# The low part of split weights: an ACTIVATE and an adding DMA in place of a VectorE subtraction

## The chip, the cores and the metric

The kernel runs on one core of one Trainium2 chip. A core has TensorE (PE, with weight loads listed apart as PEld), VectorE (DVE), ScalarE (ACT), GpSimd (POOL) and SyncE (SP), each with its own queue of instructions in order, and 16 DMA engines that serve the queues of SP, ACT and POOL. The metric is the device time of one execution in microseconds; the profile shows one execution.

## What is computed

One layer of a diffusion block in float32: a modulation, an input projection whose columns go to four mixers (mLSTM, spatial gating, convolution, S5), an output projection with residual and layer norm, and a SwiGLU feed-forward part with a second residual and layer norm. Model width 1024, 1024 latent tokens and 256 context tokens, feed-forward width 2816.

```python
z = h @ w_in_l                                  # h = x * (1 + sc1) + sh1
zc_a = hc @ w_in_l[:, :OFF_B]
zc_d = hc @ w_in_l[:, OFF_D:]
...
y = jnp.concatenate([y_a, y_b, y_c, y_d], axis=-1) @ w_out[l]
x = layer_norm(ALPHA * x + g1 * y, ln1_w[l], ln1_b[l])
x = layer_norm(ALPHA * x + g2 * swiglu(x * (1.0 + sc2) + sh2, w_ffn_in[l], w_ffn_out[l]), ln2_w[l], ln2_b[l])

def swiglu(h, w_in, w_out):
    g, u = jnp.split(h @ w_in, 2, axis=-1)
    return (jax.nn.silu(g) * u) @ w_out
```

## The kernel before

Every large product runs in the float32r format, which holds fewer bits than float32. So weights and activations are each split into a high part (the value cast to float32r) and a low part (the value minus the high part), and each product is three passes: high by high, high weight by low activation, low weight by high activation (`PASSES`). For one block k of the reduction the third matmul is therefore the first that reads the low part of the weights.

**Weights.** `wload` (L843 to L846) loads 512 KB of weights into a buffer called raw; there are two of these. `split2` (L851 to L854) makes the parts: a cast on ScalarE (L853) and a subtraction on VectorE (L854). The parts go to a tile whl, 256 KB for each part; there are four of these slots, and a slot is free again when the last product that reads it has run. In some places the parts go to a page (pg or pg3) and are twice as long, 128 x 1024. `wtile` loads and splits one tile of weights. Where a tile is one of the output weights of the feed-forward part, GpSimd first multiplies raw by the gate g2 in place (L860).

**Projections.** `projT` (L883, L885) gives columns on partitions, and its 128 columns x 8 blocks of k fill two slots; `projK` (L892) gives tokens on partitions, and a pair of its tiles (context keys, context values with gates, latent values with gates, gating) fills all four slots for as long as it runs.

**Output projection.** `out_proj` (L1183) runs for each half of the tokens over two blocks of 512 columns; each block takes four tiles of weights, two in slots and two in pages, through the two raw buffers.

**Feed-forward part.** The first four blocks of 128 columns run as plain projections. After them come nine steps of two blocks each (f = 4, 6, ... 20). In each step `gate_up2` calls `strassen` twice, for the gate weights and for the up weights: seven products of quarters in place of eight, each 12 matmuls, with the seven sums of weights from `a_sums` (L1318 to L1338). `a_sums` works in place in two raw buffers r0 and r1, each of two halves, lo and hi:

```python
yield parts(r0[:, lo])                                    # first product's weights
yield parts(r0[:, hi])                                    # second
v.tensor_tensor(r1[:, lo], r1[:, lo], r1[:, hi], op=ADD)   # L1330
v.tensor_tensor(r0[:, lo], r1[:, lo], r0[:, lo], op=SUB)   # L1331
yield parts(r0[:, lo])                                    # third
v.tensor_tensor(r0[:, hi], r0[:, hi], r0[:, lo], op=SUB)   # L1333
yield parts(r0[:, hi])                                    # fourth
yield parts(r1[:, lo])                                    # fifth
v.tensor_tensor(r1[:, lo], r1[:, hi], r0[:, lo], op=SUB)   # L1336
yield parts(r1[:, lo])                                    # sixth
yield parts(r1[:, hi])                                    # seventh
```

A sum that is written over a half of raw has to come after everything that reads the half as it was. The seven products take turns on three PSUM banks (tag mm) for the gate weights and on the others for the up weights; VectorE adds them up (L1354), the first is copied by ScalarE (L1359), SiLU runs on ScalarE (L1387), and gate times up is formed and split again (L1392 to L1394). Then the second matrix product of the step (L1451) runs with two tiles of output weights, and VectorE adds its results (L1465). After the last two steps one common second product ends the kernel.

**Order of the work.** The program is written as plain code, and a scheduler sets the order within each engine's queue; loads and splits are therefore moved ahead of the products that need them, as far as the buffers allow. `split2` asks for high priority. All loads are issued from SyncE's queue, in order, and a load into raw waits in that queue until raw is free.

Of the kernel before, what the change touches and what calls it, by code (L numbers as in the profile page):

```python
# [27 lines left out]
class Slices:  # L28
    """Small tiles cut from one larger tile."""
# [18 lines left out]
def exp_acc(e, x, shape, cut):  # L48
    """exp(x) to float32 accuracy; returns exp, expm1 of the reduced argument and the power of two."""
# [18 lines left out]
def s5_pre(e, pool, tab):  # L68
    """Everything of the S5 discretization that has one column for each (direction, pair of groups)."""
    nc = e.nc  # L70
    v, a, pe = nc.vector, nc.scalar, nc.tensor
    S = Env()
# [27 lines left out]
    # the phase of one chunk of 8 steps  # L100
# [7 lines left out]
    # powers 0..8 of a_bar: [128, dp, l]  # L108
# [22 lines left out]
    # (a_bar - 1) / lam  # L131
# [18 lines left out]
    # b_bar [128, dp, ri, p] and the same spread block-diagonally over the two groups of a pair  # L150
    S.Bb = pool.tile([128, 2, 2, 8, 16], F32, name="s5Bb")      # d, ri, P, p
# [16 lines left out]
NP = 2      # pairs of groups in a unit  # L168


def s5_unit_tables(e, S, u, tp, wp):
# [3 lines left out]
    # W = a^l b_bar, transposed to [(s p), (gi n)]  # L175
    WT = tp.tile([128, NP, 2, 2, 128], F32, name="s5W", tag="s5W")
    # columns of V, of the Toeplitz matrices and of the result: the steps of a chunk from the last to the first
# [40 lines left out]
    # kernel of the chunk by falling lag, then the Toeplitz matrices through DRAM  # L218
    BD = wp.tile([128, 4, NP, 32], F32, name="s5BD", tag="s5BD")             # (d ri), P, (gi p)
# [24 lines left out]
    for P in range(NP):  # L244
        for gi in range(2):
            # partition (s, p) takes the lags 7 - s and below of row p
            o = gi * 16 * NP * 240 + P * 240
            e.dma(M[:, P, gi, :], bass.AP(tensor=dr.tensor, offset=dr.offset + o, ap=[[16, 8], [NP * 240, 16], [1, 128]]))
    # rotation table
    Ec, Es = (tp.tile([128, 2, NP, 160], F32, name=f"s5E{x}") for x in "cs")  # L250
    for d in range(2):
# [9 lines left out]
        # cos = 1 - 2 sin(pi f)^2, sin = 2 sin(pi f) (1 - 2 sin(pi f / 2)^2)  # L261
# [66 lines left out]
def s5_out(e, Yg, y0, yT, gw, gb, wp):  # L328
    """Yg [c, 7 - t, (g q)] -> y0 (two halves), yT [128 ch, 2, 1024] with the gated linear unit"""
# [20 lines left out]
HO = (0, 2, 1, 3)       # heads as the partitions of a pair lie: (half, pair)  # L350


def mlstm_consts():
    """[104, ...] tables that depend on shapes alone: rows (head, chunk in scan order), 0..39 and 64..103"""
# [19 lines left out]
def mlstm_gates(e, Gk, page, kp):  # L374
    """Gk [128 tok, 10, 16]: gate inputs with their bias, chunks of context then latents"""
# [56 lines left out]
    G.dec = kp.tile([128, 2, 2, 10], F32, name="mdec")       # (half k), pair, direction, step  # L432
# [36 lines left out]
    G.TW = kp.tile([128, 3, 2, 40], F32, name="mTW")         # exp of: e, inter weight, -m  # L469
# [5 lines left out]
def mlstm_states(e, G, kxc, vxc, kT, vx, C, wp):  # L475
    """states before each latent chunk; context in token layout [128, 2, 256], [128, 2, 4, 65]; latents kT, vx"""
# [45 lines left out]
def mlstm_chunk(e, G, c, qT, kT, vx, hb, wp):  # L522
    """latent chunk c of both directions -> hb [128, 4, 64]"""
# [57 lines left out]
def mlstm_norm(e, hb, sq, c0, nw, sig, yT, wp, NC=4):  # L581
    """hb [128, NC, 4, 64] of chunks c0.. -> yT[:, :, tokens] = norm * weight * sigmoid(o)"""
# [23 lines left out]
def sgu_consts(e, lnb, bsb, wsT, B):  # L606
    """the bias image [(2 groups) 64 c, 2, t] from the transposed spatial weights [s, g, t]"""
# [9 lines left out]
def ln_stats(e, srcs, wp, tag, n):  # L617
    """mean and 1/std of each source row ([128, n] each) -> [128, len, 2]"""
# [12 lines left out]
def sgu_norm(e, gv, c0, wp):  # L631
    """gv [128 tok, 8, 256], chunks c0 to c0 + 3, in place"""
    mv = ln_stats(e, [gv[:, c0 + i] for i in range(4)], wp, "g", 256)
    for i in range(4):
        g = gv[:, c0 + i]
        e.nc.vector.tensor_scalar(g, g, mv[:, i, 0:1], mv[:, i, 1:2], op0=SUB, op1=MUL)


def sgu_mix(e, vn, h, wsT, B, lnw, yT, wp):
    """yT [128, 2, 1024], which holds gelu(u), times (w_s vn * ln_w + B), chunks 4 h to 4 h + 3"""  # L640
# [15 lines left out]
def conv_sums(e, wc, ws):  # L656
    """per channel: weights of the even taps plus those of the odd taps, [128, 2, 16]"""
# [5 lines left out]
def conv_taps(e, ap, j, wc, ws, bcol, p0, p1):  # L663
    """ap [128 ch, 16 rows, 96] (already twice the gated input) -> its first 64 columns, in place.

    Even and odd steps apart, with w0 the even and w1 the odd taps, and x+ one step on:
    y even = w0 * x even + w1 * x odd, y odd = (w0 + w1) * (x odd + x even+) - w0 * x even+ - w1 * x odd."""
# [16 lines left out]
def conv_norm(e, x, y, q, lnw, lnb, wp):  # L684
    """x [128 ch, 2, 16, 96], y [128 ch, 2, 1024] over it, tokens of quarter q -> silu(layer norm over the 256 channels)"""
# [24 lines left out]
PASSES = ((0, 0), (0, 1), (1, 0))       # (part of the weight, part of the activation): hi hi, hi lo, lo hi  # L710
# [10 lines left out]
def layout(x):  # L721
    """The inputs as the kernel reads them: transposed, cut into tiles, repeated; no arithmetic."""
# [5 lines left out]
    # S5: partitions (group in its pair, state)  # L728
# [11 lines left out]
    tile_ = lambda w: w.reshape(-1, 128, w.shape[1]).transpose(1, 0, 2)             # [128, k, columns]  # L740
# [21 lines left out]
def body(tc, A, out):  # L762
# [5 lines left out]
    with st:  # L768
# [18 lines left out]
        # ---- constants and small parameters  # L787
# [13 lines left out]
        # ---- modulation: the columns of sh1, sc1 for both streams  # L801
        ccol = cp.tile([128, 16], F32, name="ccol")
        a.activation(ccol, cols[:, 0:16], AF.Silu)          # (stream, k)
# [38 lines left out]
        # ---- weights: loaded, then split into two parts that float32r carries exactly  # L842
# [8 lines left out]
        def split2(hi, lo, r):  # L851
            with tc.high_priority():
                a.copy(hi, r)  # L853
                v.tensor_tensor(lo, r, hi.bitcast(F32), op=SUB)  # L854
# [670 lines left out]
```

## Time and profile before

| What | Value |
|---|---|
| median of 3 runs | 1218.36 us (1217.72 to 1219.31) |
| span of the profiled execution | 1216.7 us |
| granted TensorE clock, mean | 0.987 |
| L853, cast to the high part, 128 x 512 | 228 times, 621 ns, 140.3 us |
| L854, subtraction, pages of 128 x 1024 | 13 times, 1383 ns, 17.9 us |
| DMA queue of GpSimd | 272 packets, 0.70 MB |
| DMA queue of SyncE | 34722 packets, 100.95 MB |

The profile takes one execution apart. The span reaches from the first to the last instruction; the median is of runs without that profile. Busy time is the union of an engine's instructions. A row of a group gives the line, the engine, the operation, output and inputs with their shapes, a count after x, then busy us and mean ns, then the idle time just before the group's instructions and what ended it. A row of the timeline gives start and length in us. Matmuls are pipelined, so that one is listed as longer than the distance to the next.

### The profile page before, as it was taken

To read this page: it belongs to the slowest core of one execution; us is meant where nothing else is said; L and a number is where in the kernel's file an instruction comes from. 1 tells how busy PE (TensorE), PEld (TensorE's weight loads), DVE (VectorE), ACT (ScalarE), POOL (GpSimd) and SP (SyncE) were. 2 spreads that over 40 slices of the span, in tenths; PEclk is the share of its full clock that TensorE was granted. 3 is DMA by queue.
4 is the path that set the end of the run, shared out by engine and by line. 5 is a ranking of instruction groups with operands and counts; after the bars stand their busy time and mean duration, and the time that the engine had idled before them with its cause. 6 is when DMAs were issued, how large, how long until landed. Compare 5 with 4: busy or idle time off the path is not lost.

```text
span 1216.7 us, 15421 instructions
## 1 busy us (share of the span) xinstructions
PE 1170.0 (96%) x5803; PEld 922.9 (76%) x5803; DVE 968.2 (80%) x1902; ACT 419.5 (34%) x688; POOL 71.3 (6%) x52
## 2 busy tenths in 40 slices
PE   6999999999999999999999999999999999999987
PEld 1487788668897778678888787878787878788875
DVE  6588999988998899886866858586867676768786
ACT  1554444422336343752213132322222222323332
POOL 0010000000000000000300101010101010100110
PEclk9999999999999999999999999999999999999989
DMA  9442101121323464620111111121212121211222
GB/s 361 190 141 93 33 34 54 44 83 38 117 71 122 141 206 156 239 73 18 52 35 52 53 43 61 35 69 35 70 36 69 35 70 35 69 35 35 86 88 105
DMA packets 35213, 102.92 MB, mean 85 GB/s; under 512 B 3841, under 2 KB 8097, under 8 KB 34754
## 3 DMA queue, kind: packets, MB, share of 16 engines
q1 hardware_dynamic: 34722, 100.95, 25.2%
q8 instruction: 46, 0.75, 0.3%
q0 software_dynamic: 272, 0.70, 0.2%
q10 hardware_dynamic: 144, 0.29, 0.1%
q14 instruction: 29, 0.24, 0.1%
HBM read 96.17 MB, written 5.75 MB: 84 GB/s over the span
## 4 chain that ended last, share of the span: by engine, by line
PE 74%; DVE 17%; DMA 4%; ACT 2%; issue 2%; POOL 0%; DVEq 0%; SPq 0%; ACTq 0%; POOLq 0%
PE mm L1349 14%; PE mm L883 12%; PE mm L1451 8%; PE a L1451 6%; PE mm L1183 5%; PE b L1349 4%; PE b L1451 4%; PE b L883 4%; PE mm L892 3%; DVE whl L854 2%; PE c L1349 2%; DVE pg L1394 2%; PE c L1451 2%; DVE hs L1354 2%; DVE pg L1392 2%
## 5 line engine op out<-in xcount | busy, mean ns | idle before, releaser
L853 ACT CAST whl<-raw 128x512 fp32r<-128x512 f32 (+1 forms) x236 | 145.5, 622 | 380.6 <-PE mm L1451 153.2
L854 DVE TENSOR_TENSOR whl<-raw,whl 128x512 fp32r<-128x512 f32 (+1 forms) x236 | 165.4, 706 | 109.0 <-ACT whl L853 107.9
L883 PE MATMUL mm<-pg,whl 128*128 128x512 f32 x816 | 216.4, 404 | 0.7 <-ACT pg L1206 0.3
L883 PEld LDWEIGHTS mm<-pg,whl 128*128 128x128 f32 x816 | 146.5, 188 | 37.7 <-issue 6.1
L1349 PE MATMUL mm<-pg,whl 128*128 128x512 f32 x756 | 172.8, 389 | 0.0
L1349 PEld LDWEIGHTS mm<-pg,whl 128*128 128x128 f32 x756 | 141.9, 188 | 29.4
L1349 PE MATMUL b<-pg,whl 128*128 128x512 f32 x504 | 118.1, 389 | 0.0
L860 POOL TENSOR_TENSOR raw<-raw,g 128x1024 f32<-128x1024 f32 x22 | 61.7, 2805 | 852.4 <-DMA raw<-in_w_dram 737.0
L1349 PEld LDWEIGHTS b<-pg,whl 128*128 128x128 f32 x504 | 94.6, 188 | 19.6
L1451 PE MATMUL mm<-whl,pg 128*128 128x512 f32 x372 | 101.0, 400 | 0.0
L1451 PEld LDWEIGHTS mm<-whl,pg 128*128 128x128 f32 x372 | 72.3, 194 | 15.5
L1451 PE MATMUL a<-whl,pg 128*128 128x512 f32 x216 | 59.0, 404 | 12.8 <-DVE pg L1394 9.4
L892 PE MATMUL mm<-whl,pg 128*128 128x256 f32 (+1 forms) x448 | 63.1, 288 | 0.0
L1354 DVE TENSOR_TENSOR pg<-pg,mm 128x512 f32<-128x512 f32 x72 | 47.7, 683 | 19.0 <-PE mm L1349 18.6
L1451 PEld LDWEIGHTS a<-whl,pg 128*128 128x128 f32 x216 | 41.0, 192 | 26.1 <-DVE pg L1394 11.6
L1349 PE MATMUL c<-pg,whl 128*128 128x512 f32 x252 | 60.5, 389 | 0.0
L892 PEld LDWEIGHTS mm<-whl,pg 128*128 128x128 f32 x448 | 58.1, 190 | 1.5 <-issue 1.1
L1451 PE MATMUL b<-whl,pg 128*128 128x512 f32 x216 | 54.8, 389 | 0.0
L1349 PEld LDWEIGHTS c<-pg,whl 128*128 128x128 f32 x252 | 47.3, 188 | 9.8
L1183 PE MATMUL mm<-whl,pg 128*128 128x512 f32 x192 | 50.2, 398 | 0.3 <-DVE pg L1171 0.3
L1183 PE MATMUL mm<-pg 128*128 128x512 f32 x192 | 49.6, 401 | 0.1
L1451 PEld LDWEIGHTS b<-whl,pg 128*128 128x128 f32 x216 | 40.6, 188 | 8.4
(452 smaller groups left out, 1789.1 us busy)
## 6 DMA issues: line engine op xcount, KB each, us to landing
raw<-in_w_dram SPq DMA_DIRECT2D x66, 512.0 KB
pg<-in_wm_dram SPq DMA_DIRECT2D x16, 512.0 KB
raw<-in_wo_dram SPq DMA_DIRECT2D x16, 512.0 KB
raw<-in_wt_dram SPq DMA_DIRECT2D x14, 512.0 KB
mw<-in_w_mod_dram SPq DMA_DIRECT2D x24, 256.0 KB
vx<-in_w_mod_dram SPq DMA_DIRECT2D x24, 256.0 KB
pg<-in_x_dram SPq DMA_DIRECT2D x4, 1024.0 KB
pg<-in_w_mod_dram SPq DMA_DIRECT2D x8, 512.0 KB
```

Of the source, the lines that this page charges most:

```text
L853: a.copy(hi, r)
L854: v.tensor_tensor(lo, r, hi.bitcast(F32), op=SUB)
L860: gp.tensor_tensor(raw, raw, scale, op=MUL)
L883: pe.matmul(ps[h], lhsT=W(wi, k), rhs=rhs(hi, h, k), **f)
L892: pe.matmul(ps, lhsT=lhs(hi, k), rhs=Ws[k // 4](wi, k % 4), start=(k == 0 and n == 0), stop=(k == 7 and n == 2))
L1183: pe.matmul(ps, lhsT=Yr(hi, half, k)[:, t * 128:(t + 1) * 128], rhs=Ws[k // 2](wi, k % 2), start=(i + n == 0), stop=(i == 7 and n == 2))
L1349: pe.matmul(ps, lhsT=W[:, wi, k, :], rhs=B[b][hi][:, k], start=(k + n == 0), stop=(k == 3 and n == 2))
L1354: v.tensor_tensor(o, x, ps, op=ADD)
L1392: v.tensor_tensor(s_, c, s_, op=MUL)
L1394: v.tensor_tensor(lo(i, h), s_, hi(i, h).bitcast(F32), op=SUB)
L1451: pe.matmul(ps, lhsT=G[i][hi][:, t * 128:(t + 1) * 128], rhs=W[i // 2](wi, i % 2), start=(i + m == 0), stop=(i == n - 1 and m == 2))
```

## The change

In `split2` the subtraction on VectorE is replaced by two steps. ScalarE writes the negative of the high part into the low part's place, and a DMA issued from GpSimd's queue adds the raw weights to it (`accum_op=ADD`: the destination is read, added to and written back). This holds for all 249 splits of weights: 236 into slots and 13 into pages. The split of the activations is as before.

```diff
         def split2(hi, lo, r):
+
             with tc.high_priority():
                 a.copy(hi, r)
-                v.tensor_tensor(lo, r, hi.bitcast(F32), op=SUB)
+                a.activation(lo, hi.bitcast(F32), AF.Copy, scale=-1.0)
+                gp.dma_start(lo, r, accum_op=ADD)
```

Nothing else in the code differs but comments. Behind this place the changed kernel's lines have numbers that are higher by 2: its cast is L854, the negative L855, the DMA L856, and L1336 becomes L1338. The scheduler orders the queues anew. Three places of the same steady step (one of the later ones) show what stands where; rows give line, operation, output and inputs, and in brackets whose signals the instruction waits for (DMASW is a DMA from GpSimd's queue, DMAHW one from SyncE's).

ScalarE, from the copy of the first gate product to the first SiLU, before (the three casts are those of the fifth, sixth and seventh weight sum):

```order
L1359 COPY pg_8331<-mm_8361 128x512 [waits PE_49,Activation_49]
L853 CAST whl_8351<-raw_8334 128x512 [waits DMAHW0_49,Activation_49]
L853 CAST whl_8355<-raw_8334 128x512 [waits DVE_49,PE_49,Activation_49]
L853 CAST whl_8358<-raw_8334 128x512 [waits PE_49,Activation_49]
L1387 ACTIVATE pg_8331<-pg_8331 128x512 [waits DVE_49]
```

The same place in the changed kernel:

```order
L1361 COPY pg_8529<-mm_8566 128x512 [waits PE_49]
L854 CAST whl_8553<-raw_8532 128x512 [waits DMAHW0_49,DMASW3_49]
L855 ACTIVATE whl_8553<-whl_8553 128x512 [waits Activation_49]
L854 CAST whl_8558<-raw_8532 128x512 [waits DMASW4_49,DVE_49,PE_49]
L854 CAST whl_8562<-raw_8532 128x512 [waits DMASW5_49,PE_49]
L855 ACTIVATE whl_8558<-whl_8558 128x512 [waits Activation_49]
L855 ACTIVATE whl_8562<-whl_8562 128x512 [waits Activation_49]
L1389 ACTIVATE pg_8529<-pg_8529 128x512 [waits DVE_49]
```

Each split has two instructions on ScalarE now, and the negative of the sixth sum stands behind the cast of the seventh.

VectorE, around the sixth sum of the gate weights, before:

```order
L854 TENSOR_TENSOR whl_8348<-raw_8332,whl_8348 128x512 [waits Activation_49]
L854 TENSOR_TENSOR whl_8351<-raw_8334,whl_8351 128x512 [waits PE_49,Activation_49]
L1336 TENSOR_TENSOR raw_8334<-raw_8334,raw_8332 128x512 [waits DVE_49]
L854 TENSOR_TENSOR whl_8355<-raw_8334,whl_8355 128x512 [waits Activation_49]
L1354 TENSOR_TENSOR pg_8331<-pg_8331,mm_8388 128x512 [waits PE_49]
L854 TENSOR_TENSOR whl_8358<-raw_8334,whl_8358 128x512 [waits Activation_49]
```

The same place in the changed kernel:

```order
L1467 TENSOR_TENSOR pg_4105<-pg_4105,mm_8498 128x512 [waits PE_49]
L1338 TENSOR_TENSOR raw_8532<-raw_8532,raw_8530 128x512 [waits DMASW7_49,Activation_49]
L1356 TENSOR_TENSOR pg_8529<-pg_8529,mm_8593 128x512 [waits PE_49]
L1356 TENSOR_TENSOR pg_8529<-pg_8529,mm_8580 128x512 [waits DVE_49]
L1356 TENSOR_TENSOR pg_8529<-pg_8529,mm_8609 128x512 [waits PE_49]
```

The subtractions are gone from the queue, and the sixth sum, which waited for VectorE's own work, waits for the DMA of the fifth.

TensorE, the start of the sixth gate product, before:

```order
L1349 MATMUL mm_8434<-pg3_5229,whl_8355 128x512 [waits DVE_49,Activation_49]
L1349 MATMUL mm_8434<-pg3_5230,whl_8355 128x512
L1349 MATMUL mm_8434<-pg3_5229,whl_8355 128x512 x2
L1349 MATMUL mm_8434<-pg3_5230,whl_8355 128x512
L1349 MATMUL mm_8434<-pg3_5229,whl_8355 128x512 x2
```

The same place in the changed kernel:

```order
L1351 MATMUL mm_8639<-pg3_5303,whl_8558 128x512 [waits DVE_49,Activation_49]
L1351 MATMUL mm_8639<-pg3_5304,whl_8558 128x512
L1351 MATMUL mm_8639<-pg3_5303,whl_8558 128x512 [waits DMASW0_49]
L1351 MATMUL mm_8639<-pg3_5303,whl_8558 128x512
L1351 MATMUL mm_8639<-pg3_5304,whl_8558 128x512
```

The third matmul, the first that reads the low part, now has a wait of its own, on the DMA. On GpSimd's queue the DMAs of a step's splits stand in the order of the sums, with the two multiplications by g2 (L862) between the last of one step and the first of the next, each ahead of its own tile's DMAs. On SyncE's queue a load into raw now also waits for the DMAs that read the buffer before.

## The prediction

> **What bounds the kernel now.** I read the page's table of engines first, then the chain that ended last, then busy time by stretch. Of the engine rows the reader needs name, busy time and share.
>
> ```profile
> span 1216.7 us, 15421 instructions
> PE 1170.0 (96%) x5803; PEld 922.9 (76%) x5803; DVE 968.2 (80%) x1902; ACT 419.5 (34%) x688; POOL 71.3 (6%) x52
> PE 74%; DVE 17%; DMA 4%; ACT 2%; issue 2%; POOL 0%; DVEq 0%; SPq 0%; ACTq 0%; POOLq 0%
> 30.00:515.00 485.00, 475.26 (x2837) 367.02 (x2836) 429.63 (x1073) 213.73 (x355) 7.77 (x21) 0.99 0.33 109
> 515.00:1145.00 630.00, 616.27 (x2680) 503.83 (x2679) 461.88 (x626) 182.21 (x294) 51.18 (x18) 0.99 0.16 50
> ```
>
> In the last two rows the first pair of numbers is the stretch and its length, then busy time of PE, PEld, DVE, ACT and POOL, the granted clock, the DMA share and GB/s. TensorE is the bound: it idles 485.00 - 475.26 = 9.7 us in the mixers and projections and 630.00 - 616.27 = 13.7 us in the feed-forward part. VectorE carries 17% of the chain but is rarely what TensorE waits for. So unloading VectorE can win back part of these 23 us and no more, while a weight part that comes late is paid in full. The profiled execution is 1216.7 us of span; the median shown, 1218.36, lies 1.7 us above it, and I add every difference to the median.
>
> **What is exchanged.** Groups by shape, with mean ns after the busy time, then issues from GpSimd's queue (last number: us from issue to landing) and one such issue on POOL.
>
> ```profile
> L854 DVE TENSOR_TENSOR whl<-raw,whl 128x512 fp32r<-128x512 f32 x228 | 159.6, 706 | 108.7 <-ACT whl L853 107.6
> L853 ACT CAST pg<-raw 128x1024 fp32r<-128x1024 f32 x13 | 13.6, 1050 | 21.3 <-POOL raw L860 8.9 <-DMA raw<-in_wo_dram 7.4 <-PE a L531 4.3
> L1387 ACT ACTIVATE pg<-pg 128x512 f32<-128x512 f32 x36 | 22.8, 633 | 33.6 <-DVE pg L1354 33.1
> s5gw<-in_s_glu_w_dram POOLq DMA_DIRECT2D x1, 256.0 KB, 3.3
> gw<-in_sgu_wt_dram POOLq DMA_DIRECT2D x1, 256.0 KB, 4.5
> gbs<-in_sgu_bb_dram POOLq DMA_DIRECT2D x1, 128.0 KB, 2.7
> wc<-in_conv_t_dram POOLq DMA_DIRECT2D x1, 31.0 KB, 7.1
> 225.13 0.58 POOL L1126 DMA_DIRECT2D gw<-in_sgu_wt_dram  x1
> ```
>
> VectorE loses 228 subtractions of 0.706 us, 160 us with the few of other shapes beside. ScalarE gains as many passes of about 0.63 us (the row of an ACTIVATE on the same shape), some 145 us; at 419.5 us busy it has room. POOL gains 249 issues of about 0.58 us, 144 us. None of these sums is a term: what counts is how late the low part is ready. Before, it was the cast and the subtraction, 1.3 us. Now it is the cast, the pass, and L, the time from the issue of the adding DMA to its landing. No row shows a DMA that adds. The nearest is gw: 256 KB, 128 rows of 2 KB, same queue, 4.5 us. The other 256 KB row says 3.3; the opening's crowded queues gave 7.1 for 31 KB. An addition also reads its destination, which speaks for the upper side. I take **L = 4.5**, and keep 3.3 to 6.5.
>
> **The feed-forward blocks.** One product-of-quarters in the steady state, in order of time (start, length, engine, line):
>
> ```profile
> 891.53 19.20 PE L1349 MATMUL mm<-pg,whl 128*128 128x512 f32 x84
> 894.99 0.62 ACT L853 CAST whl<-raw 128x512 fp32r<-128x512 f32 x1
> 896.38 0.69 DVE L1336 TENSOR_TENSOR raw<-raw 128x512 f32<-128x512 f32 x1
> 897.22 0.62 ACT L853 CAST whl<-raw 128x512 fp32r<-128x512 f32 x1 [1.60 <-PE mm L1349]
> 899.95 0.62 ACT L853 CAST whl<-raw 128x512 fp32r<-128x512 f32 x1 [2.11 <-PE mm L1349]
> 900.61 0.69 DVE L854 TENSOR_TENSOR whl<-raw,whl 128x512 fp32r<-128x512 f32 x1
> 904.79 0.69 DVE L1330 TENSOR_TENSOR raw<-raw 128x512 f32<-128x512 f32 x1 [0.79 <-DMA raw<-in_w_dram]
> 910.58 2.88 PE L1349 MATMUL b<-pg,whl 128*128 128x512 f32 x12
> 915.36 0.69 DVE L1336 TENSOR_TENSOR raw<-raw 128x512 f32<-128x512 f32 x1
> 919.80 2.79 POOL L860 TENSOR_TENSOR raw<-raw,g 128x1024 f32<-128x1024 f32 x1 [55.43 <-DMA raw<-in_w_dram]
> ```
>
> 84 matmuls take 910.58 - 891.53 = 19.05 us, 0.227 each. The cast at 894.99 is that of the fifth of seven weight sums. The sixth sum (L1336) is written over the fifth's raw half, so in the changed kernel VectorE may start it only when the fifth's DMA has landed; the DVE rows of the order show that wait. Then follow, on ScalarE as its order has them, the cast of the sixth, of the seventh, and the negative of the sixth. In numbers: 894.99 + 0.62 + 0.63 = 896.24; + L; + 0.69 + 0.62 + 0.62 + 0.63 = 898.80 + L; the sixth's DMA lands at 898.80 + 2L. The sixth product's third matmul, the first to read the low part, is due after 62 matmuls, at 905.59. Late by 2L - 6.8: 2.2 us at 4.5, nothing below 3.4.
>
> The seventh's DMA lands at 899.43 + 2L and frees the second raw buffer. Its reload took 904.79 - 901.30 = 3.49 us. Two sums (1.38), cast and pass (1.25) and L again: 905.55 + 3L, for a matmul due at 910.58 + 26 x 0.227 = 916.48. That is 3L - 10.9 = 2.6, so 0.4 more. The second half of the pair (the up weights) repeats the first path, 2.2 less that 0.4. A pair costs 2(2L - 6.8) = 4.4 us, and there are nine: **+40** (0 at 3.3, 112 at 6.5). VectorE's additions that free PSUM banks stand behind the waiting sum; at 4.5 the fifth product would get its bank some 0.4 us late, inside the same stall. The scaled tile of the output weights that follows is hidden: its reload starts with the second half's sixth sum, 3.46 + 1.25 + L + 0.69 after 910.58; reload 3.75 (916.05 to 919.80), scaling 2.79, cast and pass 1.25, L: 13.2 + 2L = 22.2, when the products of that half, delayed, end at 19.05 + 2.2 and a wait of 1.35 (below) stands between. On POOL the scaling waits behind the DMA issues, 0.58 each, and they behind it, in the same cover.
>
> A stall can also cost clock. The same wait before the second matrix product is followed by two different clocks (seventh number from the end of a row's busy times: 0.72 and 1.00):
>
> ```profile
> 806.00:812.00 6.00, 5.95 (x19) 4.77 (x20) 3.86 (x7) 1.24 (x2) 0.00 (x0) 0.72 0.30 90
> 869.00:875.00 6.00, 5.13 (x23) 4.25 (x24) 5.45 (x10) 1.25 (x3) 0.00 (x0) 1.00 0.37 126
> 932.11 1.69 PE L1451 MATMUL a<-whl,pg 128*128 128x512 f32 x5 [1.35 <-DVE pg L1394]
> ```
>
> 6 x 0.28 = 1.7 us where it happens. Eighteen stalls, half of them: **+15** (0 to 31). The last row is also the gain: VectorE ends this 1.35 us wait in each of nine blocks, with subtractions of 0.69 us standing in its queue just ahead. One taken out each time: **-6**; all of it and the mixers' idle 9.7 would be -22.
>
> **Output projection.** A column block takes four slots and two pages through two raw buffers.
>
> ```profile
> 443.33 2.67 ACT L853 CAST whl<-raw 128x512 fp32r<-128x512 f32 x4 [8.13 <-issue]
> 445.40 1.69 SPq L845 DMA_DIRECT2D raw<-in_wo_dram  x2
> 450.26 1.05 ACT L853 CAST pg<-raw 128x1024 fp32r<-128x1024 f32 x1
> 453.97 2.35 DVE L854 TENSOR_TENSOR pg<-raw,pg 128x1024 fp32r<-128x1024 f32 x2
> 349.14 15.34 PE mm L892 x127
> ```
>
> The first page's low part was ready at 455.2 (453.97 and half of 2.35). Now: 443.33, ScalarE's four or six passes until the first buffer's last negative (2.5 to 3.8, say 3.1), L, reload 450.26 - 445.40 = 4.86, cast and pass 2.1, L: 453.4 + 2L, late by 2L - 1.8 = 7.2. TensorE reaches these pages about then, and SyncE's next loads queue behind the waiting reload. Three such block changes: **+22** (14 to 34). Context and token projections hold all four slots to their end; the last row gives 0.121 us per matmul, 24 of them 2.9 us. The first slot is free after 0.7, then 1.25 + L, against 2.9 + 0.9 where the next projection's low part is first read: L - 1.85 = 2.7, four times (context keys, context values, latent values, gating), **+11** (6 to 19). Elsewhere the 10.9 us (48 x 0.227) that a projection works on two slots cover it.
>
> **The last block.** Four scaled weight tiles pass two raw buffers and a scaling on POOL:
>
> ```profile
> 1141.98 0.62 ACT L853 CAST whl<-raw 128x512 fp32r<-128x512 f32 x1
> 1143.36 0.69 DVE L1336 TENSOR_TENSOR raw<-raw 128x512 f32<-128x512 f32 x1
> 1148.03 2.57 POOL L860 TENSOR_TENSOR raw<-raw,g 128x1024 f32<-128x1024 f32 x1 [95.36 <-DMA raw<-in_w_dram]
> 1151.71 1.23 DVE L854 TENSOR_TENSOR pg<-raw,pg 128x1024 fp32r<-128x1024 f32 x1 [0.56 <-ACT pg L853]
> 1156.71 2.39 POOL L860 TENSOR_TENSOR raw<-raw,g 128x1024 f32<-128x1024 f32 x1 [1.52 <-DMA raw<-in_w_dram]
> 1163.17 2.08 PE L1451 MATMUL mm<-pg,pg 128*128 128x512 f32 x4 [2.20 <-DVE pg L854]
> ```
>
> TensorE waits here already. New: 1141.98 + 1.25 + L + 0.69; + 3.98 (1144.05 to 1148.03); + 2.57 + 2.1 + L; + 3.77 (1152.94 to 1156.71); + 2.39 + 2.1 + L = 1160.8 + 3L against 1163.17: 11.2, less 2.2 counted above, **+9** (8 to 11).
>
> Sum: 40 + 15 - 6 + 22 + 11 + 9 = +91; 1218.4 + 91 = **1309 us**.
>
> **Rivals.** (a) Faster. If L is below 3.4 the nine pairs cost nothing, no stall lowers the clock, and the waits on VectorE of 1.35 us go: 9 x 1.35 = 12, and with half the mixers' idle 17; if the handovers too are covered by other products, 1201 us. For it: gbs landed in 2.7, s5gw in 3.3, and the source now lies on the chip. Against it: gw's 4.5 and the doubled reading. The Trainium skill (DMA: Bandwidth & Descriptors, Anatomy of one DMA) gives this path about 2.0 us plus bytes over 436 GB/s, an estimate of 2.6 us for 256 KB, and so this rival; the trace's 3.3 and 4.5 disagree. Chance 0.08. (b) Hidden anyway: L near 3.3, where the stalls left (14 + 6 + 8) are met by gains of up to 22: about 1219 to 1224. Chance 0.06. (c) Worse than the forecast: the additions share the DMA engines with the 512 KB reloads that they themselves release, L goes past 6.5, and the terms give 112 + 31 + 34 + 19 + 11 = 207 or more: above 1425. For it: 7.1 us under load; against: a DMA share of only 0.16 in the feed-forward part. Chance 0.12. (d) The work does not leave VectorE in effect: its queue stands still at the four sums of each half, waiting for DMAs. That is inside the forecast, and would show as wait, not as busy time.
>
> **How the numbers follow.** Forecast 0.74. Low end: 1212, below case (b) and into (a); high end: 1425, L = 6.5 with every stall. Left out: most of (a) and (c), under 0.2. A difference of 0.2%, 2.4 us, is about what a measurement here can tell. Faster 0.08, same 0.04, slower 0.88.
>
> **What would show it.** DVE busy down by about 180 us, ACT up by about 150. Adding DMAs landing in 4 to 5 us. TensorE waiting on DMA at the sixth product of each half, 2 us, and on page tiles in the output projection, 7 us. Wrong if TensorE's idle stays below 60 us, if adding DMAs land under 3.4 us, or if the stalls lie in the third or fourth product instead.

## The result, and the profile after

The changed kernel takes 1312.49 us (median of 4 runs, 1311.84 to 1315.33) against 1218.04 us for the kernel before in the same series (4 runs, 1214.99 to 1219.31): a ratio of 1.0778, 95% interval 1.0757 to 1.08. The forecast was 1309.

First the page after: the engines, GpSimd's DMA queue, and two groups that carry the change (columns as before).

```profile
span 1310.9 us, 16179 instructions
...
PE 1197.3 (91%) x5803; PEld 929.2 (71%) x5803; DVE 777.5 (59%) x1653; ACT 559.6 (43%) x937; POOL 278.2 (21%) x301
...
q0 software_dynamic: 36128, 69.52, 31.0%
...
L856 POOL DMA_DIRECT2D whl<-raw x236 | 203.4, 918 | 863.9 <-ACT whl L855 451.8
...
L1338 DVE TENSOR_TENSOR raw<-raw 128x512 f32<-128x512 f32 x18 | 12.5, 693 | 118.1 <-DMA whl<-raw 118.1
```

The work moved as it should: VectorE lost 191 us, ScalarE gained 140, GpSimd 207. But VectorE now stands 118 us at the sixth sum. TensorE's idle time, span less busy, grew from 1216.7 - 1170.0 = 46.7 to 1310.9 - 1197.3 = 113.6 us; the other 27 us of the 94 are busy time of the same 5803 matmuls. The clock explains some 13 of these (mean granted clock 0.987 before and 0.978 after: 1310.9 x 0.022 - 1216.7 x 0.013). The rest goes with the number of stops, as worked out further below: the last matmul ahead of a wait is listed as longer than one within a row.

Where do they lie? The next view is busy time by stretch, cut at the same places of the program (the counts in brackets differ by up to 15 matmuls, since the order does): up to the output projection; the output projection; the first blocks of the feed-forward part; seven Strassen steps; the last two steps with the end. Before:

```profile
0.00:370.10 370.10, 354.37 (x2102) 259.47 (x2103) 320.63 (x893) 144.33 (x260) 9.60 (x30) 0.99 0.31 106
370.10:495.30 125.20, 122.41 (x685) 98.57 (x684) 111.93 (x266) 57.12 (x78) 0.00 (x0) 0.99 0.45 148
495.30:641.00 145.70, 142.60 (x644) 114.39 (x643) 113.81 (x117) 56.07 (x79) 14.33 (x4) 1.00 0.26 85
641.00:1081.50 440.50, 427.73 (x1850) 349.86 (x1849) 320.07 (x464) 117.90 (x196) 36.85 (x14) 0.99 0.17 51
1081.50:1216.70 135.20, 122.92 (x529) 100.58 (x527) 101.81 (x168) 44.08 (x75) 10.53 (x4) 0.96 0.23 78
```

After:

```profile
0.00:390.90 390.90, 358.65 (x2117) 263.64 (x2118) 293.59 (x847) 169.06 (x308) 51.35 (x78) 0.98 0.48 130
390.90:534.90 144.00, 129.46 (x676) 101.49 (x675) 92.71 (x235) 70.45 (x100) 19.24 (x23) 0.95 0.71 188
534.90:686.60 151.70, 144.54 (x637) 115.44 (x636) 94.31 (x97) 70.59 (x103) 29.08 (x26) 0.98 0.50 127
686.60:1156.10 469.50, 436.39 (x1850) 347.45 (x1850) 221.51 (x340) 188.69 (x324) 143.00 (x141) 0.99 0.56 118
1156.10:1310.90 154.80, 128.22 (x529) 101.19 (x527) 75.41 (x137) 60.81 (x105) 35.48 (x34) 0.95 0.53 126
```

The stretches grow by 20.8, 18.8, 6.0, 29.0 and 19.6 us, 94.2 in all. In each, idle time is the length less the first busy number: in the seven steps 440.50 - 427.73 = 12.8 before and 469.50 - 436.39 = 33.1 after.

Now one half of a steady step in the timeline after, in order of time. The product at 1021.87 starts the gate weights' seven, the cast at 1025.27 is the fifth sum's.

```profile
1021.87 14.21 PE L1351 MATMUL mm<-pg,whl 128*128 128x512 f32 x62
...
1025.27 0.62 ACT L854 CAST whl<-raw 128x512 fp32r<-128x512 f32 x1
1025.92 0.63 ACT L855 ACTIVATE whl<-whl 128x512 fp32r<-128x512 f32 x1
...
1026.85 0.85 POOL L856 DMA_DIRECT2D whl<-raw  x1 [2.35 <-ACT whl L855]
...
1030.24 0.69 DVE L1338 TENSOR_TENSOR raw<-raw 128x512 f32<-128x512 f32 x1 [7.49 <-DMA whl<-raw]
...
1032.98 1.74 POOL L856 DMA_DIRECT2D whl<-raw  x2 [5.28 <-PE mm L1351]
...
1036.04 0.86 POOL L856 DMA_DIRECT2D whl<-raw  x1 [1.32 <-ACT whl L855]
...
1036.30 5.29 PE L1351 MATMUL mm<-pg,whl 128*128 128x512 f32 x22 [0.22 <-DMA whl<-raw]
...
1037.24 0.86 POOL L856 DMA_DIRECT2D whl<-raw  x1 [0.34 <-ACT whl L855]
...
1043.32 0.69 DVE L1332 TENSOR_TENSOR raw<-raw 128x512 f32<-128x512 f32 x1 [3.13 <-DMA raw<-in_w_dram]
...
1049.79 0.50 PE L1351 MATMUL b<-pg,whl 128*128 128x512 f32 x1 [2.31 <-DMA whl<-raw]
```

In the view by tile, the two reloads of raw in these 29 us (duration of the issue, then first and last start):

```profile
L845 SPq DMA_DIRECT2D raw<-in_w_dram x2: 328/328/328, 1031.0 to 1038.0; - x2
```

This is the chain that the prediction described. The fifth's negative ends at 1026.55, its DMA is issued by 1027.70, and the sixth sum can start at 1030.24: L = 3.7 us, issue included. The sixth's and seventh's DMAs follow (1032.98), and after 62 matmuls the sixth product waits a mere 0.22 us. But the seventh's DMA also frees the second raw buffer. Its reload is issued at 1038.0 and is there at 1043.3, 5.3 us where 3.49 were planned: the additions for the first two sums of the next half, issued at 1036.04 and 1037.24, move on the same DMA engines, whose busy share is 0.86 in this stretch (last number but one):

```profile
1036.00:1043.30 7.30, 7.08 (x32) 5.80 (x32) 2.24 (x4) 2.19 (x4) 1.71 (x2) 1.00 0.86 178
```

This holds for all seven steps: the reload with two additions issued just ahead of it takes 4.1 to 6.4 us, the other half's reload, with none ahead of it, 3.5 to 3.8. So the third sum comes late, and the third product of the up weights waits 2.31 us.

### The profile page after: what moved, and what is told of

Read it like the earlier page. It is cut to its first block, busy times and chain, and to the rows that moved or that the text cites. A ratio compares the mean times of both kernels' runs of the same rounds, so it can differ in the third digit from the quotient of the medians.

```text
span 1310.9 us, 16179 instructions
## 1 busy us (share of the span) xinstructions
PE 1197.3 (91%) x5803; PEld 929.2 (71%) x5803; DVE 777.5 (59%) x1653; ACT 559.6 (43%) x937; POOL 278.2 (21%) x301
## 3 DMA queue, kind: packets, MB, share of 16 engines
q0 software_dynamic: 36128, 69.52, 31.0%
q1 hardware_dynamic: 34722, 100.95, 22.8%
## 5 line engine op out<-in xcount | busy, mean ns | idle before, releaser
L856 POOL DMA_DIRECT2D whl<-raw x236 | 203.4, 918 | 863.9 <-ACT whl L855 451.8
L854 ACT CAST whl<-raw 128x512 fp32r<-128x512 f32 (+1 forms) x236 | 142.8, 619 | 423.5 <-PE mm L1453 110.4
L885 PE MATMUL mm<-pg,whl 128*128 128x512 f32 x816 | 217.8, 406 | 5.9 <-DVE pg L1210 4.0
L1351 PE MATMUL mm<-pg,whl 128*128 128x512 f32 x756 | 176.3, 391 | 9.1 <-DMA whl<-raw 7.7
L855 ACT ACTIVATE whl<-whl 128x512 fp32r<-128x512 f32 (+1 forms) x236 | 145.1, 629 | 4.5
L1351 PE MATMUL b<-pg,whl 128*128 128x512 f32 x504 | 125.6, 401 | 16.9 <-DMA whl<-raw 16.2
L1338 DVE TENSOR_TENSOR raw<-raw 128x512 f32<-128x512 f32 x18 | 12.5, 693 | 118.1 <-DMA whl<-raw 118.1
L1351 PE MATMUL c<-pg,whl 128*128 128x512 f32 x252 | 64.7, 405 | 9.3 <-DMA whl<-raw 8.8
L894 PE MATMUL mm<-whl,pg 128*128 128x256 f32 (+1 forms) x448 | 66.1, 294 | 6.3 <-DMA whl<-raw 6.3
L862 POOL TENSOR_TENSOR raw<-raw,g 128x1024 f32<-128x1024 f32 x22 | 55.6, 2528 | 16.7 <-DMA raw<-in_w_dram 15.3
```

What stands on the lines that cost most here:

```text
L855: a.activation(lo, hi.bitcast(F32), AF.Copy, scale=-1.0)
L856: gp.dma_start(lo, r, accum_op=ADD)
L862: gp.tensor_tensor(raw, raw, scale, op=MUL)
L885: pe.matmul(ps[h], lhsT=W(wi, k), rhs=rhs(hi, h, k), **f)
L894: pe.matmul(ps, lhsT=lhs(hi, k), rhs=Ws[k // 4](wi, k % 4), start=(k == 0 and n == 0), stop=(k == 7 and n == 2))
L1351: pe.matmul(ps, lhsT=W[:, wi, k, :], rhs=B[b][hi][:, k], start=(k + n == 0), stop=(k == 3 and n == 2))
```

## The experiments

Each ran in a series beside the kernel before; differences are between medians of one series, and ratios have their 95% interval. "Steps" are the seven Strassen steps, 440.5 us before and 469.5 after, as cut above; each such length is from one profiled execution.

**Which splits cost.** The adding DMA for the Strassen sums alone, and for the other tiles alone; elsewhere VectorE subtracts as before. The new argument says whether a split takes the negative and the DMA; the diff is that of the first run, and the second has the two values exchanged.

```diff
-                split2(x[:, 0], x[:, 1], r)
+                split2(x[:, 0], x[:, 1], r, True)
-                split2(hl[:, 0], hl[:, 1], raw[:, k:k + n])
+                split2(hl[:, 0], hl[:, 1], raw[:, k:k + n], False)
```

> The negative and the adding DMA only for the sums of weights in the Strassen steps (126 of the 249 splits); all other tiles are split by VectorE as before. Theory: the nine steps' own stalls stay and nothing else. In the changed kernel's trace the program's landmarks move by 29.0 us over the first seven steps and by 15.5 over the last two, so 1218 + 44 = about 1262, at least 1250. Rival (contention: additions of all kinds slow each other and the reloads): half of the additions cost clearly less than this, below 1245, and the two halves of the change together come to far less than its whole.

> The opposite: the negative and the adding DMA for all tiles of weights (projections, output projection, scaled output weights), VectorE's subtraction for the Strassen sums. Theory: opening and mixers 20 us, output projection 20, first blocks of the feed-forward part 6, last block 4, by the shifts of the landmarks in the changed kernel, so about 1268; the steps of the feed-forward part keep their old length of 62.9 us. Rival (the scaled tiles of output weights are not hidden in a step, but carry the steps' loss): steps of 65 us or more and 1280 or more.

The sums alone took 1280.98 us against 1220.58, ratio 1.0496 (1.0472 to 1.052), +60.4; the tiles alone 1259.11, ratio 1.0316 (1.0284 to 1.0348), +38.5. Together 98.9, close to the whole's 94.5: the two add up, with no large cost that needs both. But each missed its number: 60 us where 44 were forecast, and 38 where 50 were. The steps say why, with the sums alone:

```profile
645.40:1125.20 479.80, 437.36 (x1850) 348.68 (x1849) 243.62 (x367) 172.43 (x296) 119.46 (x113) 0.99 0.46 100
```

and with the tiles alone:

```profile
690.60:1121.40 430.80, 423.17 (x1850) 347.50 (x1849) 304.70 (x436) 134.91 (x224) 58.52 (x42) 1.00 0.27 69
```

The sums lengthen the steps by 39 us, and the tiles, which in a step are the scaled output weights, shorten them by 10. In the whole change 29 is what is left. A gain was hidden in it.

**The gain by itself.** The adding DMA only for the 28 splits of scaled output weights of the first seven steps; and the same 28 on GpSimd with no DMA.

```diff
-            return wtile(A["w2"][c, :, f0:f0 + 2], 2, 512, scale=bc(g2[:, None, cs_], [128, 2, 512]), pool_tag=tag)
+            return wtile(A["w2"][c, :, f0:f0 + 2], 2, 512, scale=bc(g2[:, None, cs_], [128, 2, 512]), pool_tag=tag, other=4 <= f0 < NFF - 4)
```

> VectorE subtracts everywhere but in the 28 splits of scaled output weights of the first seven Strassen steps, where the negative and the adding DMA stay. The run with all tiles by DMA had steps of 57 to 62 us, 11 us shorter in all than before, and lost its 50 us ahead of the steps. Theory (these tiles are covered in a step, and VectorE's shorter queue ahead of the second product is worth 1.6 us a step): 1219 - 11 = about 1208, at least faster than before by 4 us. Rival (the shorter steps there came from a cooler clock after slower mixers, or from the order of the last blocks): 1215 to 1225.

> GpSimd subtracts for the 28 splits of scaled output weights of the first seven Strassen steps, VectorE does all others; no DMA adds anything. Theory (in these steps it counts only that VectorE's queue is shorter, how the low part is made does not): as the run that gave these 28 splits to the adding DMA, 1206 us within 3. Rival (GpSimd's 1.5 us beside VectorE's work slow VectorE, as its subtraction of the sums may have): 1211 or more.

1206.16 us against 1220.75, ratio 0.989 (0.9869 to 0.991); and 1207.5 against 1220.36, ratio 0.989 (0.9873 to 0.9906). **Both are faster than both kernels**, by 1.1%. How the low part is made there makes no difference; that four subtractions a step are gone from VectorE's queue does. The steps of the first run:

```profile
643.80:1069.70 425.90, 421.38 (x1849) 346.25 (x1848) 303.16 (x436) 134.59 (x224) 59.67 (x42) 1.00 0.27 70
```

and in its timeline the wait ahead of one second matrix product, 1.35 us before:

```profile
865.03 1.43 PE L1456 MATMUL a<-whl,pg 128*128 128x512 f32 x5 [0.56 <-DVE pg L1399]
```

14.6 us shorter than before: 8.3 of idle time and 6.3 of busy time. Of the latter 5.1 are clock: before, it drops three times in the steps behind that wait, at 1.7 us each, and here not once.

**The chain in the sums.** One run takes the fifth's DMA out of the sixth sum's way; the other leaves the DMA to the first four sums and gives the three at the chain's head back to VectorE (all tiles too). Their edits, one after the other:

```diff
-            v.tensor_tensor(r1[:, lo], r1[:, hi], r0[:, lo], op=SUB)
-            yield parts(r1[:, lo])
+            v.tensor_tensor(r0[:, lo], r1[:, hi], r0[:, lo], op=SUB)
+            yield parts(r0[:, lo])
...
-            yield parts(r0[:, hi])
-            yield parts(r1[:, lo])
+            yield parts(r0[:, hi], True)
+            yield parts(r1[:, lo], False)
```

> The whole change, but the sixth sum is written over r0's lower half (the third sum, long read) in place of r1's. So it waits no longer for the fifth's DMA, and r1, whose last reader is the seventh, comes free some 4 us earlier; r0 comes free later instead. Theory (the steps lose by the chain fifth DMA, sixth sum, sixth DMA, seventh DMA, reload of r1): the two stalls of a step that lie on it, at the sixth product and at the third of the second half, go, and with them most of the 43 us that the sums cost: 1312 down to 1270 to 1285, steps of 62 to 63.5 us in place of 67.1. Rival (every adding DMA is late for its own product or slows the reloads, whatever it is chained to): 1300 or more.

> The negative and the adding DMA only for the first four of the seven weight sums of each product (72 of the 249 splits); VectorE subtracts the other three and all tiles. Theory (a chain of three landings, fifth, sixth or seventh, and the third sum of the next half, crosses from one half into the next; no single one is late): r1 comes free as early as before, and the third sum's low part, one landing later than before, is still 5 us ahead of its matmul: 1213 to 1226, where all seven cost 60 us. Rival (each addition is late for its own product, or slows the reloads): four sevenths of 60, 1245 or more.

The first run took 1308.37 us, ratio 1.072 (1.0696 to 1.0744): by its own number the theory had failed. TensorE's waits in the steps (us, times, longest) in the changed kernel:

```profile
PE b L1351 <- DMA whl<-raw: 9.1, 7, 2.3
PE c L1351 <- DMA whl<-raw: 8.8, 4, 3.3
PE mm L1351 <- DMA whl<-raw: 4.9, 7, 1.5
```

and in this run:

```profile
PE a L1453 <- DMA whl<-raw: 11.1, 7, 1.6
PE a L1453 <- ACT pg L1395: 9.9, 7, 2.0
PE b L1351 <- DMA whl<-raw: 3.5, 5, 0.9
```

The waits inside the products did go, from 22.8 us to about 5, but the second matrix product now waits for its scaled tile and for ScalarE: r0 comes free later, and what is loaded into it is late instead. In all, idle time in the steps fell only from 33.1 to 28.3 us, and the clock took that back: its drops cost 13.6 us in place of 5.1 (1.7 each, as shown further below; mean granted clock 0.97, third number from the end, in place of 0.99).

```profile
693.00:1163.10 470.10, 441.77 (x1850) 353.68 (x1850) 243.18 (x340) 192.62 (x324) 143.46 (x141) 0.97 0.56 118
```

The waiting was for the most part shifted, not saved. The second run answers the question: 1219.95 against 1218.65 us, ratio 1.0006 (0.9987 to 1.0025), with 72 adding DMAs in place of the 126 that cost 60 us alone; the idle time in its steps is 12.8 us, as before. Four sevenths of the additions cost nothing; the loss needs the last three sums and the landing they put ahead of the reload. Here it is shown that the chain costs, not an addition as such.

**What the landing costs.** The same change, but the DMA copies the raw weights and adds nothing: the addition is left out.

```diff
-                gp.dma_start(lo, r, accum_op=ADD)
+                gp.dma_start(lo, r)
```

> The whole change, but the DMA copies the raw weights over the low part and does not add: the addition is left out, the negative is overwritten. All waits and orders stay. Theory (what costs is a DMA in the path at all: its issue on GpSimd, descriptors, transfer, completion): landing about as late, 3 us and more, and 1295 to 1312. Rival (the addition itself, which reads the destination and keeps DMA engines longer, makes L and slows the reloads): DMA share in the feed-forward part falls from 0.55 towards 0.35, landings below 2.7 us, and 1270 or less.

1252.08 us (1238.92 to 1254.95), ratio 1.0243 (1.0199 to 1.0287), and steps of 438.0 us. DMA issues of the changed kernel, with KB and median us to landing:

```profile
whl<-raw POOLq DMA_DIRECT2D x228, 256.0 KB, 3.4
...
pg<-raw POOLq DMA_DIRECT2D x13, 512.0 KB, 5.5
```

and from this run's page its queue and the same issues:

```profile
q0 software_dynamic: 36128, 69.52, 18.0%
...
whl<-raw POOLq DMA_DIRECT2D x228, 256.0 KB, 2.3
...
pg<-raw POOLq DMA_DIRECT2D x13, 512.0 KB, 3.8
```

Some 1.1 us less to landing takes away the whole loss of the steps, as a chain that counts L two or three times and has a threshold near 3.4 would have it. So the rival was right that the addition makes L: at 2.3 the stalls in the products are 0.5 us in seven steps. Which part comes from the shorter landing and which from DMA engines that are less busy (share in the steps 0.42, not 0.56) this run can't separate.

**The output projection and the mixers by themselves.** The flag on the tiles of the output projection alone, and on those of the projections ahead of it alone.

```diff
-                Ws = {kk: wtile(A["wo"][c, kk], 2, 512, pool_tag=tag) for kk, tag in ((3, None), (1, None), (2, page), (0, page))}
+                Ws = {kk: wtile(A["wo"][c, kk], 2, 512, pool_tag=tag, other=True) for kk, tag in ((3, None), (1, None), (2, page), (0, page))}
```

> The negative and the adding DMA only for the 16 tiles of the output projection (24 of the 249 splits, 8 of them pages); VectorE subtracts all others. Theory (raw stays taken until the DMA lands, so that the next block's pages are loaded and split late): the 20 to 22 us between the first and the last matmul of the output projection in the changed kernel arise here alone, so 1240, with waits on page tiles. Rival (the block changes are late only because the mixers ahead are, or other work fills them): below 1230.

> The negative and the adding DMA only for the tiles of the projections ahead of the output projection; VectorE subtracts all others. Theory: the 20 us that the changed kernel is late at the first matmul of the output projection arise here alone, half of it in the first 90 us, where the weights' own loads fill the DMA engines, half at the four handovers of all slots: 1240. Rival (the later stages make up for part of it, since they are then further ahead with their loads): 1225 to 1232.

1242.41 us, ratio 1.0171 (1.0153 to 1.0188): 22 us, with the waits on page tiles in place. The mixers: 1234.12 us, ratio 1.0107 (1.0085 to 1.013), 13.8 us, between the two numbers. What lacks to 20.8 fits the program's very first tile, which this run left to VectorE and which is looked at below. TensorE's waits in the first run's output projection:

```profile
PE mm L1188 <- DMA pg<-raw: 8.1, 5, 3.3
PE mm L1188 <- DMA whl<-raw: 3.1, 4, 1.2
```

**The ScalarE pass without the DMA, and GpSimd in place of both.** First VectorE adds what the DMA added:

```diff
-                gp.dma_start(lo, r, accum_op=ADD)
+                v.tensor_tensor(lo, r, lo.bitcast(F32), op=ADD)
```

> ScalarE still writes the negative of the high part, but VectorE adds the raw weights to it in place of the DMA. This keeps the added ScalarE pass and takes the DMA away. Theory (the loss is the time until the DMA lands, through the waits chained to it): the low part is ready one ScalarE pass (0.63 us) later than before and not 4 us, less than every slack named in the prediction, so about 1218 to 1230 us, and VectorE's waits on DMA at the sixth sum (118 us in the changed kernel) vanish. Rival (the loss is ScalarE's 249 extra passes and the order of its queue): still 1280 us or more.

1238.57 us, ratio 1.0141 (1.0106 to 1.0175): 18 us, past the 1230 where the theory ended and far below the rival's 1280. The steps are as before (440.3 us). The profiled execution, the slowest of the four, is 23.2 us longer than that before, and 12.4 of these lie in the first blocks of the feed-forward part (503.4 to 661.5, 158.1 us against 145.7), some 6 of them by the clock (0.96 there, 1.00 before). There, and not in the steps, one pass more is paid for, be it by the later low part or by ScalarE's longer queue; the run can't tell these apart.

Then GpSimd subtracts, in one run for all splits, in the other for the sums of the nine steps and the scaled tiles of the first seven:

```diff
-                a.activation(lo, hi.bitcast(F32), AF.Copy, scale=-1.0)
-                gp.dma_start(lo, r, accum_op=ADD)
+                gp.tensor_tensor(lo, r, hi.bitcast(F32), op=SUB)
```

> GpSimd subtracts, in place of the negative and the DMA. GpSimd's multiplication of 128 x 1024 takes 2.4 to 2.8 us, so half of that, some 1.3 us, for a 128 x 512 subtraction, against VectorE's 0.7 and the 4 us until the DMA lands; busy time of GpSimd some 320 + 60 us. Theory (what counts is how late the low part is): 0.6 us later than before, which no slack named in the prediction notices, and the gain of 6 to 17 us from VectorE's shorter queue shows: 1205 to 1225. Rival (the work taken off VectorE is of no use to TensorE, or GpSimd's and VectorE's work slow each other): 1225 to 1260.

> No DMA adds anything: GpSimd subtracts the sums of the nine Strassen steps and the scaled tiles of the first seven, VectorE everything else. The run with all splits on GpSimd had steps 11 us shorter in all, and lost 50 us ahead of them, where projections wait for the 1.5 us subtraction. Theory: those 50 us do not arise, the 11 us stay: about 1208. Rival (the steps are shorter only because what goes before is longer, with loads further ahead): 1215 to 1230.

All splits on GpSimd: 1261.67 us, ratio 1.0343 (1.0306 to 1.0381), a plain miss. The first Strassen product starts at 690.1 in place of 641.0, so all of the loss lies ahead of the steps, which are 10 us shorter than before. In the steps alone: 1213.13 against 1220.75 us, ratio 0.994 (0.9918 to 0.9961), faster, though less so than with 28 splits, and between the numbers of theory and rival. The groups of the first of the two runs, GpSimd's subtraction and VectorE's sum of two raw halves:

```profile
L855 POOL TENSOR_TENSOR whl<-raw,whl 128x512 fp32r<-128x512 f32 x228 | 337.4, 1487 | 614.8 <-ACT whl L854 576.4 <-DVE pg L1355 27.8 <-issue 7.1
L1332 DVE TENSOR_TENSOR raw<-raw 128x512 f32<-128x512 f32 x18 | 21.9, 1215 | 8.1 <-POOL whl L855 7.2
```

The subtraction takes 1.49 us, twice VectorE's 0.71, and the sum beside it 1.22 in place of 0.69. Of the 49 us ahead of the steps 30 arise up to the output projection, 11 in it and 8 behind it; which projections lose them was not taken apart.

Not tried: a third raw buffer or more slots. Either might take the wait on the landing away; whether the memory has room for them beside the rest is not shown here.

## Why the prediction was right, point by point

**The bound held.** TensorE paid for the late low parts; VectorE's 191 us of relief bought some 10 us (the steps with the tiles alone) inside a loss ten times as large.

**L** was taken as 4.5 from gw's row; in the steps it is 3.7, inside the range. From issue to landing the median is 3.4, where 4 to 5 had been named as the sign for the forecast, and less than 3.4 as one against it. The estimate worked out from the Trainium skill's formula for the path (DMA: Bandwidth & Descriptors, Anatomy of one DMA) was 2.6 us. The copies' 2.3 lie a little below it; the additions' 3.4 lie above it.

**Stalls in the steps, +40.** Right in sum, wrong in place. Three more rows give the ends of the two kinds over all nine steps: sixth product of the first half (mm), of which 1036.30 above is the shortest, and third product of the second half (b or c):

```profile
770.77 5.29 PE L1351 MATMUL mm<-pg,whl 128*128 128x512 f32 x22 [1.52 <-DMA whl<-raw]
782.77 5.30 PE L1351 MATMUL b<-pg,whl 128*128 128x512 f32 x22 [0.81 <-DMA whl<-raw]
1232.96 2.58 PE L1351 MATMUL b<-pg,whl 128*128 128x512 f32 x10 [3.32 <-DMA whl<-raw]
```

The sixth product waits 0.22 to 1.52 us, 6.3 in nine steps, where 2.2 each had been put. 2L - 6.8 at 3.7 is 0.6: the formula was right, L too large. The third product of the second half waits 0.81 to 3.32 us, 20.4 in all, where 0.4 each had been put. 3L - 10.9 is 0.2 at 3.7; the reload's 5.3 in place of 3.49 adds 1.8. The second half's sixth product has 4.6, and the ninth step's third 1.4. Together 32.7 against 40. **The step that failed** is the reload at its old price: contention had been dismissed by a DMA share of 0.16, which was the share before the additions existed. It was 0.56 after. Rival (c) was wrong in size but had this mechanism, and the sign named against the forecast, stalls at a third product, came true: 21.8 of the 32.7 us.

**Clock, +15.** Right in sum by luck, wrong in place, and a second step that failed. Cut into slices of 1 us, the granted clock of both traces falls to 0.50 for some 3.4 us at a time, now and then for twice that; 3.4 us cost the 1.7 that the prediction had. But half of eighteen stalls had been taken to end so, and the nine steps have four such drops, and three before the change: 2 us more, not 15. The clock's loss lies elsewhere, where it had no term: 5 us more in the output projection, 3 more ahead of it, 3 more in the first blocks of the feed-forward part. In the whole program it grows by 14 us.

The 436.39 - 427.73 = 8.7 us by which busy time grows in the seven steps are not clock, then: three drops before, three after. They are the ends of stops. By the last two rows above 22 matmuls up to a stop are listed with 5.30 us and 10 with 2.58, so 0.227 for each and 0.3 over; TensorE stops 42 times in these steps, 14 times before, and 28 x 0.3 is 8.4. By this estimate the 25 stops of the stalls above cost some 7 us beside their 32.7 of waiting, which is 40 as forecast.

**Gain, -6.** Too small: 14.6 us in seven steps when it stands alone. The wait of 1.35 fell to 0.56, the 0.48 ahead of it went in six of the seven, and the clock came back; only the first had been counted, by half. In the whole change less of it is left: the waits ahead of the second product fall from 12.7 to 9.2 us. Together with the stalls and the clock, the nine steps were to cost 49 us; from the first Strassen matmul (641.0 and 686.6) to the start of the last product (1157.6 and 1247.8) it grew by 44.6.

**Output projection, +22.** 18.8 in the whole change, 22 alone. Its make-up was different: 11.8 us of idle time (2.8 before, 14.5 after) and 7.1 of busy time, 5 of it clock, in place of three stalls of 7.2. The longest wait for a page is 3.5.

**Handovers, +11.** 20.8 arose. The waits for additions at the token and context projections are 6.8 us (context 4.2, latent values 0.6, gating 2.0), less than the 11, with one drop of the clock among them. Not priced was the opening: the first matmul of the context projections is 9.8 us later than before (88.81 and 79.05). Its largest wait is for the first tile, whose addition was issued into the opening's full DMA engines:

```profile
33.47 1.79 POOL L856 DMA_DIRECT2D whl<-raw  x2 [30.82 <-DMA pg<-in_wm_dram]
40.80 0.80 PE L887 MATMUL a<-pg,whl 128*128 128x256 f32 x2 [4.22 <-DMA whl<-raw]
```

Over 7 us to landing, as wc's row had shown. **Elsewhere covered** by other work: no, the first blocks of the feed-forward part lost 6.0 us. **Last block, +9:** 4, the rest of the 94.2 behind the start of that last product (90.2 late already); its tiles are late as expected, by less.

So 91 against 94 rests partly on errors that cancel: steps 4.5 and last block 5 too dear, output projection 3 too dear, opening 10 and first blocks 6 too cheap. And it was in good part luck: with the measured 3.7 for L the prediction's own formulas give some 52 us (stalls 11, clock 15, gain -6, output projection 17, handovers 7, last block 8). An L that was too long stood in for the slower reload and the opening. Rivals (a) and (b) asked for L below 3.4, which only the copying run has, and there the steps do come out as before.

## What to carry to other kernels

A split on a spare engine is worth what its lateness leaves. Ask first which instruction overwrites or reloads the buffer that the new step still reads: a landing that was harmless once is counted two or three times when each landing releases the next. And ask which few instructions stand right ahead of the wait on the path; moving 28 of 249 gained 1.1%, moving all of them lost 7.8%. A contention estimate has to use the traffic after the change.

## What the runs showed of the hardware

**The clock drops in steps of one size, and after short waits.** In a drop the granted clock (last number but two) is 0.50, here within one before and within one after:

```profile
806.90:810.10 3.20, 3.20 (x9) 2.52 (x8) 2.10 (x4) 0.97 (x2) 0.00 (x0) 0.50 0.38 95
1050.70:1054.00 3.30, 3.30 (x10) 2.52 (x9) 0.83 (x2) 0.06 (x1) 0.00 (x0) 0.50 0.54 91
```

In the seven steps there are three drops before, each behind a wait of 1.35 us, while the same wait in the other four steps has none; three after, behind waits of 2.31, 2.40 and 3.31 us; and none in the run with 28 splits by DMA, where no wait is longer than 0.7. In the changed kernel's last step 3.32 us were waited without a drop, so the length of one wait does not decide it. The Trainium skill (TensorE: Matmul & The Clock Gate, Part 1) has the slow clock come after an idle window of about 3.4 us; these runs lose clock with shorter waits.

**An adding DMA is a dearer DMA.** The same 69.52 MB in the same 36128 packets took 31.0% of the DMA engines' span when added and 18.0% when copied (of spans of 1310.9 and 1249.0 us).

**GpSimd slows VectorE when both read two tensors of the on-chip memory:** 1.22 us on average for a sum of 0.69. One such sum, from the run with all splits on GpSimd, ends 0.54 us after the subtraction beside it:

```profile
827.99 1.34 POOL L855 TENSOR_TENSOR whl<-raw,whl 128x512 fp32r<-128x512 f32 x1 [1.44 <-ACT whl L854]
828.27 1.60 DVE L1332 TENSOR_TENSOR raw<-raw 128x512 f32<-128x512 f32 x1
```

The Trainium skill (SBUF — State Buffer, SBUF: two separate sides) says that an operation of VectorE with two inputs there and one of GpSimd that reads there lock each other out; the rows agree.
